# The gate projection of two pairs of each SwiGLU stage by seven products of quarters

## The chip, the cores and the metric

The kernel runs on one core of a Trainium2 chip, in one launch. The metric is the device time of one execution in microseconds. A core has five engines that run side by side, each with its own in-order row of instructions: TensorE (PE; its weight loads are PEld), VectorE (DVE), ScalarE (ACT), GpSimd (POOL) and SyncE (SP), which here only issues DMAs.

## The reference, cut to what matters

```python
D_MODEL, SEQ, DEPTH, D_FF = 1024, 512, 2, 2816

def swiglu_ffn(x, g, w_gate, w_up, w_down):
    h = rmsnorm(x, g)
    return (jax.nn.silu(h @ w_gate) * (h @ w_up)) @ w_down

    for i in range(DEPTH):
        x = x + 0.5 * swiglu_ffn(x, ffn1_norm[i], ffn1_w_gate[i], ffn1_w_up[i], ffn1_w_down[i])
        h = rmsnorm(x, mix_norm[i])
        if i % 2 == 0:
            ...
        else:
            ...
        x = x + 0.5 * swiglu_ffn(x, ffn2_norm[i], ffn2_w_gate[i], ffn2_w_up[i], ffn2_w_down[i])
    return rmsnorm(x, final_norm)
```

All is fp32. So there are four SwiGLU stages, and a mixer (attention of several kinds; left out above) behind the first and behind the third.

## The kernel before

**Numbers in two halves.** An fp32 operand is cut into a high part that TensorE takes and the rest, a low part: `h` by a copy on ScalarE, `l = src - h` on VectorE (`cut`, L326 to L331, or `parts`, L708 to L710). `mm3` (L333 to L336) makes one product from three matmuls: high by high (L334), high by low (L335), low by high (L336). The normalised activations are cut once a stage (tiles `xg`); weights are cut as they come, from `raw` tiles into `wh` and `wl`, four buffers each.

**A stage.** The 2816 columns are 11 pairs `k` of 256, in three groups, `GROUPS` = (0,4), (4,8), (8,11). For each pair of a group `gate_up` (L758 on) makes gate and up; behind the group's pairs `proj_T` makes its part of the down projection, in four steps of 256 rows, each ending in two `update`s of x (L585; `x7` is the last). Each step takes two units of down weights, cut at L329 and L330.

**A pair.** The first one or two pairs of a stage go by `gate_up_pair` and aren't touched. In every other pair the gate is made directly: two units of 512 rows, each 2 x 4 products of 512 columns, 48 matmuls in all, into two PSUM banks of tag `psT`. Behind it come `rb` (the row of 1/rms of the norm), a product with it on VectorE (L780), the Silu on ScalarE (L781) and a product on GpSimd (L782). The up projection goes by `seven` (L688 on), a scheme of the Strassen kind: the 1024 x 256 weights and the activations are split in quarters, and seven products of quarters take the place of eight. It makes four additions of weight quarters (L725 to L728, tiles `s`), and four cuts: h1 (512 columns, product 1), h2 (1024; products 2 and 4), u and v (1024 each, cut from the sums; products 3, 5 and 6, 7). Each product is 4 x 3 matmuls of 256 columns, 84 in all, run in the order 1, 2, 3, 5, 6, 7, 4 into four banks of tag `psG`. Two copies on ScalarE (L742, L746) and seven operations on VectorE (L744 to L756) combine them. The activations' sums (`Sums`, tiles `t7h`, `t7l`) are made once a stage. At the end up is multiplied by gate (L785, L787), and the result is cut for the down projection (`split`, L508 and L509).

**The ahead work.** `cut_ahead` cuts the mixers' weights while the first three stages run their down projections, into which it is woven: load a unit into `craw`, cut it into `ch` (ScalarE, L329) and `cl` (VectorE, L330), store both to DRAM. Each of its loads is held back by a copy on GpSimd (L305) of one column of the x tile updated last, into the `craw` tile:

```python
            if gate:
                nc.gpsimd.tensor_copy(raw[:, 0:1], mark[0])
```

**What sets the order.** The program is written in the order of the loops; a scheduler at build time then sets each engine's row by data and buffers, and the engines run their rows in order, waiting on semaphores. So an instruction that waits holds back all behind it on its engine. All loads and stores of weights are issued in order by SyncE. Buffers of one tag are handed out by the order in which they come free.

Of the kernel before, what the change touches and what calls it, by code (L numbers as in the profile page):

```python
# [20 lines left out]
P = 128  # L21
# [6 lines left out]
GROUPS = ((0, 4), (4, 8), (8, 11))  # L28
PSUM_BUFS = {'B': 4, 'S': 3, 'T': 4, 'C': 2, 'X': 2, 'G': 4}
SB_BUFS = {'xg': 18, 'f': 36, 'm': 8, 'p': 8, 'pt': 9}  # L30
AHEAD = 3
YB = 5
TRAIL = (8, 4)
# [32 lines left out]
def hybrid_kernel(tc, x_in, positions, ffn1_norm, ffn1_w_gate, ffn1_w_up, ffn1_w_down, mix_norm,  # L66
# [4 lines left out]
    with ExitStack() as ctx:  # L71
# [11 lines left out]
        def ps_tile(tag):  # L83
            return psp.tile([P, S], F32, tag=tag, bufs=PSUM_BUFS[tag], name=nm("ps" + tag))

        def tile_(tag, dt=F32R):
            return sb.tile([P, S], dt, tag=tag, bufs=SB_BUFS[tag], name=nm(tag))

# [168 lines left out]
        def wunit(src, a, b, rows=False, key=None, tag=("raw", "wh", "wl")):  # L257

            n = a * b
            if key in cut_units:
                res = []
                for part, t in zip(cut_units[key], tag[1:]):
                    w = sb.tile([P, 1024], F32R, tag=t, bufs=W_BUFS, name=nm(t))
                    nc.sync.dma_start(w[:, :n].bitcast(F32), part)
                    res.append(w[:, :n].rearrange("p (a b) -> p a b", a=a))
                return res
            h, l = cut(load_raw(src, a, b, rows, tag[0], RAW_BUFS), n, tag[1:], W_BUFS)
            return (h[:, :n].rearrange("p (a b) -> p a b", a=a), l[:, :n].rearrange("p (a b) -> p a b", a=a))  # L270
# [414 lines left out]
                        self.term[n][c] = tuple(t[:, sl] for t in self.norm.xg[c + 4 * i])  # L685
                    yield

        def seven(w, f0, sums, z):  # L688

# [37 lines left out]
            for t, ns in ((u, (3, 5)), (v, (6, 7))):  # L729
                h, l = new("wh", F32R, W_BUFS), new("wl", F32R, W_BUFS)  # L730
                parts(h, l, t)
                for i, n in enumerate(ns):
                    st[n] = quarter(h, i), quarter(l, i)
            bank = [ps_tile("G") for _ in range(4)]
            q = {n: bank[i % 4][:, i // 4 * 256:i // 4 * 256 + 256] for i, n in enumerate((1, 2, 3, 5, 6, 7, 4))}
            k1, k3, k6 = (sb.tile([P, 256], F32, tag="k7", bufs=6, name=nm("k7")) for _ in range(3))
            a, b = slice(0, 256), slice(256, 512)
# [20 lines left out]
        def gate_up(wg, wu, k, norm, sums, at):  # L758

            f0 = 256 * k  # L760
            if k < (1 if norm.source is None else 2):
                gate_up_pair(wg, wu, f0, norm, k == 0, sums.work, at)
                return
            psg = [ps_tile("T"), ps_tile("T")]
            for hf in range(2):
                h, l = wunit(wg[hf * 512:(hf + 1) * 512, f0:f0 + 256].rearrange("(c p) f -> p c f", p=P), 4, 256)
                if hf:
                    norm.rstd()
                for f in range(2):
                    if hf and f:  # L770
                        norm.finish()
                    for c in range(4):
                        xh, xl = norm.xg[hf * 4 + c]
                        mm3(psg[f], h[:, c, f * P:(f + 1) * P], l[:, c, f * P:(f + 1) * P], xh, xl,
                            hf == 0 and c == 0, hf == 1 and c == 3)
            rb = norm.rstd_row()
            gs, up = [], [tile_("p", F32) for _ in range(2)]
            for f in range(2):
                g = tile_("p", F32)
                nc.vector.tensor_mul(g, psg[f], rb)  # L780
                nc.scalar.activation(g, g, AF.Silu)  # L781
                nc.gpsimd.tensor_mul(g, g, rb)  # L782
                gs.append(g)
            seven(wu, f0, sums, up)
            nc.vector.tensor_mul(up[0], up[0], gs[0])  # L785
            at.append(split(up[0]))
            nc.vector.scalar_tensor_tensor(up[1], up[1], -1.0, gs[1], op0=ALU.mult, op1=ALU.mult)  # L787
            at.append(split(up[1]))
            mark[0] = at[-1][0][:, 0:1].bitcast(F32)
# [817 lines left out]
```

## Time and profile before

| | |
|---|---|
| median of 3 runs | 2017.05 us (2015.41 to 2019.02) |
| the profiled execution | 2017.72 us |
| its span, first to last instruction | 2016.0 us |
| mean granted clock of TensorE in it | 0.995 of full speed |

The profile is of one execution of its own. The page gives busy times over the span, the chain of work that ended last, and the costliest groups of instructions. A timeline lists an engine's instructions by start, with their length, their line and tiles (out<-in), and in brackets how long the engine had been idle before and what released it. A window gives, for a stretch, the time for which each engine was busy. The eight places that the change touches lie at 146 (stage 1, pair 4), 280 (pair 8), 828 and 960 (stage 2), 1191 and 1321 (stage 3), 1779 and 1906 us (stage 4).

### The profile page before, as it was taken

What the parts mean: (1) busy time and instruction counts of PE and PEld (TensorE: products, weight loads), DVE (VectorE), ACT (ScalarE), POOL (GpSimd) and SP (SyncE); (2) the same over time, 40 slices, a digit from 0 to 9 for tenths busy, and PEclk for the clock granted to TensorE, in tenths of its full rate; (3) what the DMA queues carried; (4) which work ended last, traced back from release to release, by engine and by line L of the source; (5) the groups of instructions that cost most, each with busy time, mean ns of one, the idle gap of its engine ahead of it and who ended that gap; (6) DMA issues with size and microseconds to landing.
All of it is one profiled execution on the core that took longest, in us unless ns stands there. A gap on an engine that the chain in (4) does not pass through costs nothing.

```text
span 2016.0 us, 30453 instructions
## 1 busy us (share of the span) xinstructions
PE 1955.9 (97%) x11575; PEld 1731.1 (86%) x11575; DVE 1391.0 (69%) x2448; ACT 905.8 (45%) x1570; POOL 335.6 (17%) x418
## 2 busy tenths in 40 slices
PE   8999999999989999999999999999999999999998
PEld 7888888898877788788888888888999788889898
DVE  6767767535787786676768758566698787567464
ACT  6434334325677644333445434334346764334143
POOL 1201111023234011111101111010112202011012
PEclk9999999999999999999999999999999999999999
DMA  5386493933100235737543493423542232323321
GB/s 168 94 264 193 137 281 125 335 128 123 46 11 12 64 109 170 246 105 251 182 155 96 144 305 105 135 87 106 197 143 95 78 95 83 116 84 105 104 85 63
DMA packets 216962, 273.58 MB, mean 136 GB/s; under 512 B 25368, under 2 KB 190960, under 8 KB 216816
## 3 DMA queue, kind: packets, MB, share of 16 engines
q1 hardware_dynamic: 209888, 265.23, 40.7%
q10 hardware_dynamic: 6736, 6.37, 1.0%
q8 instruction: 91, 1.49, 0.3%
q14 instruction: 55, 0.45, 0.1%
q0 software_dynamic: 192, 0.04, 0.0%
HBM read 221.72 MB, written 49.87 MB: 135 GB/s over the span
## 4 chain that ended last, share of the span: by engine, by line
PE 52%; DVE 8%; DMA 2%; issue 2%; ACT 1%; POOL 0%; ACTq 0%; POOLq 0%; DVEq 0%; SPq 0%
PE psB L334 6%; PE psB L335 6%; PE psB L336 6%; PE psT L334 6%; PE psT L336 6%; PE psT L335 6%; PE psG L334 4%; PE psG L336 4%; PE psG L335 4%; DMA craw<-in_od_w_in_dram 2%; DVE f L1432 1%; DVE sm L1431 1%; PE psC L964 1%; PE psS L336 1%; PE psS L334 1%
## 5 line engine op out<-in xcount | busy, mean ns | idle before, releaser
L330 DVE TENSOR_TENSOR wl<-raw,wh 128x1024 fp32r<-128x1024 f32 (+1 forms) x210 | 270.2, 1288 | 82.1 <-ACT wh L329 79.3
L329 ACT ACTIVATE wh<-raw 128x1024 fp32r<-128x1024 f32 (+1 forms) x210 | 207.9, 992 | 196.5 <-PE psB L335 119.7
L334 PE MATMUL psT<-xg,wh 128*128 128x512 f32 x704 | 275.1, 391 | 0.0
L335 PE MATMUL psT<-xg,wh 128*128 128x512 f32 x704 | 274.2, 390 | 0.0
L336 PE MATMUL psT<-xg,wl 128*128 128x512 f32 x704 | 274.1, 390 | 0.0
L334 PE MATMUL psB<-f,wh 128*128 128x512 f32 x656 | 255.5, 390 | 0.0
L335 PE MATMUL psB<-f,wh 128*128 128x512 f32 x656 | 255.3, 389 | 0.0
L336 PE MATMUL psB<-f,wl 128*128 128x512 f32 x656 | 255.2, 389 | 0.0
L782 POOL TENSOR_TENSOR p<-p,p 128x512 f32<-128x512 f32 x78 | 132.4, 1700 | 702.5 <-ACT p L781 652.6
L334 PE MATMUL psG<-t7h,wh 128*128 128x256 f32 x624 | 178.9, 287 | 13.7 <-ACT k L742 7.9
L335 PE MATMUL psG<-t7l,wh 128*128 128x256 f32 x624 | 177.3, 284 | 0.0
L336 PE MATMUL psG<-t7h,wl 128*128 128x256 f32 x624 | 176.8, 284 | 0.0
L336 PEld LDWEIGHTS psT<-xg,wl 128*128 128x128 f32 x704 | 132.2, 188 | 27.7
L334 PEld LDWEIGHTS psT<-xg,wh 128*128 128x128 f32 x704 | 132.3, 188 | 26.6
L335 PEld LDWEIGHTS psT<-xg,wh 128*128 128x128 f32 x704 | 132.3, 188 | 26.3
L334 PE MATMUL psB<-wh,xg 128*128 128x256 f32 x512 | 148.5, 290 | 0.3 <-DMA wh<-cuth 0.2
L336 PEld LDWEIGHTS psB<-f,wl 128*128 128x128 f32 x656 | 123.1, 188 | 25.7
L336 PE MATMUL psB<-wh,xg 128*128 128x256 f32 x512 | 145.1, 283 | 0.0
L334 PEld LDWEIGHTS psB<-f,wh 128*128 128x128 f32 x656 | 123.2, 188 | 25.3
L335 PEld LDWEIGHTS psB<-f,wh 128*128 128x128 f32 x656 | 123.2, 188 | 25.1
L335 PE MATMUL psB<-wl,xg 128*128 128x256 f32 x512 | 144.7, 283 | 0.0
L710 DVE TENSOR_TENSOR wl<-s,wh 128x1024 fp32r<-128x1024 f32 x78 | 101.8, 1307 | 57.3 <-ACT wh L709 57.3
(307 smaller groups left out, 4602.1 us busy)
## 6 DMA issues: line engine op xcount, KB each, us to landing
raw<-in_ffn_w_down_dram SPq DMA_DIRECT2D x168, 256.0 KB, 3.3
raw<-in_ffn_w_gate_dram SPq DMA_DIRECT2D x80, 512.0 KB, 4.1
raw<-in_ffn_w_up_dram SPq DMA_DIRECT2D x80, 512.0 KB, 4.1
cuth<-ch SPq DMA_DIRECT2D x40, 512.0 KB, 4.5
cutl<-cl SPq DMA_DIRECT2D x40, 512.0 KB, 4.8
wl<-cutl SPq DMA_DIRECT2D x40, 512.0 KB, 3.6
wh<-cuth SPq DMA_DIRECT2D x40, 512.0 KB, 4.4
craw<-in_od_w_in_dram SPq DMA_DIRECT2D x16, 512.0 KB, 5.2
```

What stands on the lines that cost most here:

```text
L329: pin(nc.scalar.activation(h[:, :n], raw[:, :n], AF.Copy))
L330: pin(nc.vector.tensor_sub(l[:, :n], raw[:, :n], h[:, :n].bitcast(F32)))
L334: nc.tensor.matmul(ps, lh, rh, start=start, stop=False)
L335: nc.tensor.matmul(ps, lh, rl, start=False, stop=False)
L336: nc.tensor.matmul(ps, ll, rh, start=False, stop=stop)
L710: nc.vector.tensor_sub(l, src, h.bitcast(F32))
L782: nc.gpsimd.tensor_mul(g, g, rb)
L964: nc.tensor.matmul(job["accs"][0][:, j * P:512], v(j), hl[j][part], start=first, stop=last)
L1431: nc.vector.max(out=m8, in_=bd[i])
L1432: nc.vector.match_replace(out=bd[i], in_to_replace=m8, in_values=bd[i], imm_value=-3e38)
```

## The change

In pairs 4 and 8, the first pairs of the second and third group, of each stage, the gate is made by `seven` as well, with four banks of tag `psT`. Its result then lies in two tiles `p`, of which the second has its sign turned; so the product with `rb` takes a factor -1 there (L786 of the changed kernel). Silu and the GpSimd product are as before. What `seven` reads of the activations is there already. The weights of a gate are loaded in the same two transfers of 512 KB.

```diff
--- before.py
+++ after.py
@@ -28,6 +28,7 @@
 GROUPS = ((0, 4), (4, 8), (8, 11))
 PSUM_BUFS = {'B': 4, 'S': 3, 'T': 4, 'C': 2, 'X': 2, 'G': 4}
 SB_BUFS = {'xg': 18, 'f': 36, 'm': 8, 'p': 8, 'pt': 9}
+GATE_SEVEN = (4, 8)
 AHEAD = 3
 YB = 5
 TRAIL = (8, 4)
@@ -685,7 +686,7 @@
                         self.term[n][c] = tuple(t[:, sl] for t in self.norm.xg[c + 4 * i])
                     yield
 
-        def seven(w, f0, sums, z):
+        def seven(w, f0, sums, z, tag="G"):
 
 
 
@@ -731,7 +732,7 @@
                 parts(h, l, t)
                 for i, n in enumerate(ns):
                     st[n] = quarter(h, i), quarter(l, i)
-            bank = [ps_tile("G") for _ in range(4)]
+            bank = [ps_tile(tag) for _ in range(4)]
             q = {n: bank[i % 4][:, i // 4 * 256:i // 4 * 256 + 256] for i, n in enumerate((1, 2, 3, 5, 6, 7, 4))}
             k1, k3, k6 = (sb.tile([P, 256], F32, tag="k7", bufs=6, name=nm("k7")) for _ in range(3))
             a, b = slice(0, 256), slice(256, 512)
@@ -761,23 +762,30 @@
             if k < (1 if norm.source is None else 2):
                 gate_up_pair(wg, wu, f0, norm, k == 0, sums.work, at)
                 return
-            psg = [ps_tile("T"), ps_tile("T")]
-            for hf in range(2):
-                h, l = wunit(wg[hf * 512:(hf + 1) * 512, f0:f0 + 256].rearrange("(c p) f -> p c f", p=P), 4, 256)
-                if hf:
-                    norm.rstd()
-                for f in range(2):
-                    if hf and f:
-                        norm.finish()
-                    for c in range(4):
-                        xh, xl = norm.xg[hf * 4 + c]
-                        mm3(psg[f], h[:, c, f * P:(f + 1) * P], l[:, c, f * P:(f + 1) * P], xh, xl,
-                            hf == 0 and c == 0, hf == 1 and c == 3)
+            if k in GATE_SEVEN:
+                psg = [tile_("p", F32) for _ in range(2)]
+                seven(wg, f0, sums, psg, "T")
+            else:
+                psg = [ps_tile("T"), ps_tile("T")]
+                for hf in range(2):
+                    h, l = wunit(wg[hf * 512:(hf + 1) * 512, f0:f0 + 256].rearrange("(c p) f -> p c f", p=P), 4, 256)
+                    if hf:
+                        norm.rstd()
+                    for f in range(2):
+                        if hf and f:
+                            norm.finish()
+                        for c in range(4):
+                            xh, xl = norm.xg[hf * 4 + c]
+                            mm3(psg[f], h[:, c, f * P:(f + 1) * P], l[:, c, f * P:(f + 1) * P], xh, xl,
+                                hf == 0 and c == 0, hf == 1 and c == 3)
             rb = norm.rstd_row()
             gs, up = [], [tile_("p", F32) for _ in range(2)]
             for f in range(2):
-                g = tile_("p", F32)
-                nc.vector.tensor_mul(g, psg[f], rb)
+                g = psg[f] if k in GATE_SEVEN else tile_("p", F32)
+                if k in GATE_SEVEN and f:
+                    nc.vector.scalar_tensor_tensor(g, psg[f], -1.0, rb, op0=ALU.mult, op1=ALU.mult)
+                else:
+                    nc.vector.tensor_mul(g, psg[f], rb)
                 nc.scalar.activation(g, g, AF.Silu)
                 nc.gpsimd.tensor_mul(g, g, rb)
                 gs.append(g)
```

A place gives up 48 matmuls of 512 columns, two cuts of 1024 on ScalarE and VectorE, and two VectorE products from PSUM (L780). It gets 84 matmuls of 256 columns, a cut of 512 and three of 1024, four additions of 512, two copies of 256 on ScalarE, seven combining operations of 256 on VectorE, and two products of 512 from SBUF. Lines of the changed kernel are one higher up to the middle of `seven`'s end and eight higher behind the gate.

The build sets the rows anew. VectorE, stage 3, the end of the down projection of group 1 and pair 4; `cl` is the ahead cut, `wl<-raw` and `wl<-s` cuts of weights and of their sums, `x_99` the last x tile, `k` and `p` the combining operations. Before (`psT` tiles are the gate's results, `wl_11914`, `wl_11924` and `wl_11928` are the up projection's h2, u and v):

```order
L585 SCALAR_TENSOR_TENSOR x_99<-psB_11744,x_99 128x512
L710 TENSOR_TENSOR wl_11914<-raw_11907,wh_11913 128x1024
L710 TENSOR_TENSOR wl_11924<-s_2409_11917,wh_11923 128x1024
L330 TENSOR_TENSOR cl_12699<-craw_11829,ch_12698 128x1024
L780 TENSOR_TENSOR p_11897<-psT_11833,p_10878 128x512
L725 TENSOR_TENSOR s_2444_12125<-raw_12113,raw_12115 128x512
L728 TENSOR_TENSOR s_2445_12126<-raw_12113 128x512
L726 TENSOR_TENSOR s_2445_12126<-s_2444_12125,raw_12113 128x512
L780 TENSOR_TENSOR p_11901<-psT_11834,p_10878 128x512
L727 TENSOR_TENSOR s_2444_12125<-s_2445_12126,raw_12115 128x512
L710 TENSOR_TENSOR wl_11928<-s_2410_11918,wh_11927 128x1024
```

Now (`wl_12234`, `wl_12244` and `wl_12248` are the up projection's h2, u and v; `psT` tiles are the gate's seven products):

```order
L331 TENSOR_TENSOR cl_13019<-craw_12085,ch_13018 128x1024
L751 TENSOR_TENSOR k_2455_12123<-psT_12117,k_2453_12121 128x256
L711 TENSOR_TENSOR wl_12234<-raw_12227,wh_12233 128x1024
L752 TENSOR_TENSOR p_12089<-k_2455_12123,k_2454_12122 128x256
L754 TENSOR_TENSOR k_2455_12123<-psT_12118,k_2455_12123 128x256
L788 TENSOR_TENSOR p_12089<-p_12089,p_11134 128x512
L755 TENSOR_TENSOR p_12090<-psT_12120,k_2455_12123 128x256
L757 TENSOR_TENSOR p_12090<-psT_12119,k_2455_12123 128x256
L711 TENSOR_TENSOR wl_12244<-s_2464_12237,wh_12243 128x1024
L786 SCALAR_TENSOR_TENSOR p_12090<-p_12090,p_11134 128x512
L711 TENSOR_TENSOR wl_12248<-s_2465_12238,wh_12247 128x1024
```

The cuts of h2 and u stood ahead of the ahead cut and now stand behind it, with five of the gate's combining operations and its first product with `rb` among them.

VectorE, stage 1, the same part of the program, before (`cl` are three ahead cuts, `wl_1461` the gate's second unit, `wl_1503` the up projection's h1):

```order
L330 TENSOR_TENSOR wl_1461<-raw_1458,wh_1460 128x1024
L330 TENSOR_TENSOR cl_1369<-craw_1329,ch_1368 128x1024
L585 SCALAR_TENSOR_TENSOR x_98<-psB_1335,x_98 128x512
L585 SCALAR_TENSOR_TENSOR x_99<-psB_1336,x_99 128x512
L330 TENSOR_TENSOR cl_1416<-craw_1376,ch_1415 128x1024
L330 TENSOR_TENSOR cl_2292<-craw_1423,ch_2291 128x1024
L710 TENSOR_TENSOR wl_1503<-raw_1498,wh_1502 128x512
```

Now (`wl_1437`, `wl_1447` and `wl_1451` are the gate's h2, u and v):

```order
L711 TENSOR_TENSOR wl_1437<-raw_1430,wh_1436 128x1024
L331 TENSOR_TENSOR cl_1369<-craw_1329,ch_1368 128x1024
L711 TENSOR_TENSOR wl_1447<-s_283_1440,wh_1446 128x1024
L586 SCALAR_TENSOR_TENSOR x_98<-psB_1335,x_98 128x512
L586 SCALAR_TENSOR_TENSOR x_99<-psB_1336,x_99 128x512
L331 TENSOR_TENSOR cl_1416<-craw_1376,ch_1415 128x1024
L711 TENSOR_TENSOR wl_1451<-s_284_1441,wh_1450 128x1024
L745 TENSOR_TENSOR p_1426<-psT_1455,k_293_1458 128x256
L749 TENSOR_TENSOR k_294_1459<-psT_1457,k_294_1459 128x256
L331 TENSOR_TENSOR cl_2356<-craw_1423,ch_2355 128x1024
```

A cut of the gate's sums now stands ahead of the last two x updates, and the last ahead cut stands behind the gate's first combining operations.

## Rows read from the trace of the kernel before

**Rows 1.** The page: busy time of each engine; shares of the chain that ended last

```profile
PE 1955.9 (97%) x11575; PEld 1731.1 (86%) x11575; DVE 1391.0 (69%) x2448; ACT 905.8 (45%) x1570; POOL 335.6 (17%) x418
PE 52%; DVE 8%; DMA 2%; issue 2%; ACT 1%; POOL 0%; ACTq 0%; POOLq 0%; DVEq 0%; SPq 0%
```

**Rows 2.** Windows: stretch, length, busy PE, PEld, DVE, ACT, POOL (count); clock, DMA, GB/s

```profile
146.25:157.13 10.88, 10.88 (x49) 9.01 (x48) 3.81 (x5) 2.76 (x3) 0.18 (x1) 1.00 1.03 348
157.13:173.17 16.04, 12.40 (x85) 11.63 (x84) 14.02 (x19) 7.51 (x10) 3.13 (x2) 0.89 0.77 260
290.54:302.64 12.10, 10.58 (x86) 10.17 (x84) 10.99 (x16) 6.45 (x9) 3.53 (x2) 1.00 0.92 276
838.54:853.92 15.38, 10.84 (x86) 10.22 (x84) 12.86 (x17) 7.30 (x10) 3.14 (x2) 1.00 0.52 193
971.28:985.69 14.41, 11.92 (x85) 11.42 (x84) 13.09 (x17) 5.46 (x9) 3.76 (x2) 0.88 0.47 161
1201.74:1214.91 13.17, 10.59 (x85) 10.17 (x84) 12.52 (x16) 5.76 (x9) 3.76 (x2) 1.00 0.64 220
1778.74:1789.62 10.88, 10.88 (x50) 9.01 (x48) 6.24 (x8) 2.73 (x3) 0.17 (x1) 1.00 0.16 48
1789.62:1799.69 10.07, 10.07 (x86) 10.07 (x84) 7.57 (x11) 4.92 (x7) 2.95 (x2) 1.00 0.24 60
```

**Rows 3.** Timeline, VectorE, stage 3, pair 4: start, duration, what, [idle before, releaser]

```profile
1202.25 1.23 DVE L330 TENSOR_TENSOR cl<-craw,ch 128x1024 fp32r<-128x1024 f32 x1 [3.65 <-ACT ch L329]
1205.20 1.79 DVE L726 TENSOR_TENSOR s<-s,raw 128x512 f32<-128x512 f32 x1
1207.51 0.68 DVE L727 TENSOR_TENSOR s<-s,raw 128x512 f32<-128x512 f32 x1
1208.11 1.21 DVE L710 TENSOR_TENSOR wl<-s,wh 128x1024 fp32r<-128x1024 f32 x1
1215.19 0.42 DVE L754 TENSOR_TENSOR p<-psG,k 128x256 f32<-128x256 f32 x1
1215.52 0.41 DVE L756 TENSOR_TENSOR p<-psG,k 128x256 f32<-128x256 f32 x1
```

**Rows 4.** The same stretch: ScalarE and GpSimd

```profile
1201.15 1.06 ACT L329 ACTIVATE ch<-craw 128x1024 fp32r<-128x1024 f32 x1 [3.81 <-DMA craw<-in_od_w_out_dram]
1194.70 1.06 POOL L305 COPY craw<-x 128x1 f32<-128x1 f32 x1 [12.26 <-DVE x L585]
1204.82 1.61 POOL L782 TENSOR_TENSOR p<-p,p 128x512 f32<-128x512 f32 x1 [9.06 <-ACT p L781]
```

**Rows 5.** Timelines, stage 2, pair 4 (838 on) and pair 8 (971 on): VectorE and TensorE

```profile
840.14 1.23 DVE L330 TENSOR_TENSOR cl<-craw,ch 128x1024 fp32r<-128x1024 f32 x1 [6.55 <-ACT ch L329]
848.16 0.39 PE L334 MATMUL psG<-t7h,wh 128*128 128x256 f32 x1 [2.72 <-ACT k L742]
972.19 1.22 DVE L330 TENSOR_TENSOR cl<-craw,ch 128x1024 fp32r<-128x1024 f32 x1 [4.06 <-DMA cutl<-cl]
979.44 0.38 PE L334 MATMUL psG<-t7h,wh 128*128 128x256 f32 x1 [2.25 <-ACT k L742]
```

**Rows 6.** TensorE after that wait, and the window of it (columns as in Rows 2)

```profile
982.69 0.41 PE L334 MATMUL psG<-t7h,wh 128*128 128x256 f32 x1
982.90 0.41 PE L335 MATMUL psG<-t7l,wh 128*128 128x256 f32 x1
981.00:983.00 2.00, 1.76 (x9) 1.47 (x8) 2.00 (x4) 0.00 (x0) 0.00 (x0) 0.50 0.17 29
```

**Rows 7.** Timelines, stage 1, pair 4: VectorE, SyncE's issues, TensorE

```profile
145.94 1.28 DVE L585 SCALAR_TENSOR_TENSOR x<-psB,x 128x512 f32<-128x512 f32 x2
155.51 1.23 DVE L330 TENSOR_TENSOR cl<-craw,ch 128x1024 fp32r<-128x1024 f32 x1 [5.80 <-ACT ch L329]
147.99 1.87 SPq L699 DMA_DIRECT2D raw<-in_ffn_w_up_dram  x2
163.97 0.39 PE L334 MATMUL psG<-xg,wh 128*128 128x256 f32 x1 [2.72 <-ACT wh L709]
```

## The prediction

> **What bounds the kernel now.** The page first: TensorE is busy 97% of the span, and no other engine is above 69% except its own weight loads [rows 1]. So the first price of an edit is the TensorE time that it removes, and the second is the idle time that the other 3% hold. The chain that ended last says whose idle time that is: after TensorE's 52% the largest share is VectorE's 8% [rows 1]. The windows then show where it sits. I cut the eight places that the change touches (pairs 4 and 8 of four stages) into the gate projection and the up projection behind it. The gate takes 10.88 us with TensorE busy all of it, at all eight places (the first and one later stand there) [rows 2]. The up projection takes 10.07 us where nothing disturbs it, in the last stage [rows 2]; pair 8 of stage 3 and pair 8 of stage 4 are like it. I call these three the quiet places. At the other five it takes 16.04, 12.10, 15.38, 14.41 and 13.17 us for the same 84 products [rows 2]: 20.7 us are lost behind these five gates, and VectorE is busy 11.0 to 14.0 us there against 7.57. The five are the places beside `cut_ahead`, which cuts the mixer's weights during the down projections of the first three stages.
>
> The timeline of one such place, pair 4 of stage 3, shows the mechanism. GpSimd's small copy that frees the next ahead load waits for the last x update of the down projection and runs at 1194.70. The load lands and ScalarE's half of the cut runs at 1201.15, after 3.81 us of waiting for it [rows 4]. VectorE's half stands in its in-order row and starts at 1202.25 after 3.65 us of idling [rows 3]. All that is queued behind it on VectorE, cuts of the up projection's weights among it, waits too. I call the end of this ahead cut C: 1203.48 here; 841.37 and 973.41 for pairs 4 and 8 of stage 2 [rows 5]; 156.74 for pair 4 of stage 1 [rows 7]. The up projection ends 11.4, 12.6, 12.3 and 16.4 us after its C [rows 2]. C hangs on an x update and a load, not on how fast the gate is multiplied.
>
> **Part 1, TensorE.** The gate loses 48 products of 512 columns, 48 x 0.2267 = 10.88 us, and gets 84 of 256, 84 x 0.1199 = 10.07 us, both from the undisturbed windows [rows 2]. That is 0.81 us a place and 6.5 us for eight. Weight loads are busy all of the 10.07 us [rows 2], so the smaller products don't run at half the time of the larger. The page "TensorE: Matmul & The Clock Gate" of the Trainium skill (section Back-to-back issue gap) puts the isolated gap at N/2.4 + 2.5 ns, so 215.8 and 109.2 ns; the saving would be 1.19 us a place and 9.5 us for eight. The rows are 0.2267 and 0.1199 us, the trace disagrees, and the rows decide.
>
> **Part 2, VectorE's and ScalarE's load.** By the spacing of VectorE's rows, a 1024 cut costs 1.13 us, a 512 operation 0.60, a 256 one 0.33 [rows 3] (the cut from its length of 1.21 less the 0.08 by which a 512 operation of 0.68 exceeds 0.60). A place loses two cuts and two 512 products (3.5 us), and gets three cuts of 1024 and one of 512, four additions, seven combining operations and two 512 products: 4.0 + 2.4 + 2.3 + 1.2 = 9.9 us. So VectorE has 6.4 us more a place, on an engine with idle time; ScalarE gets about 2.4 us (one 1024 cut of 1.06 [rows 4], a 512 cut of about half, two short copies), hidden everywhere by its 45% load [rows 1]. GpSimd and the loads do what they did.
>
> **Part 3, the quiet places.** VectorE is busy 6.24 + 7.57 = 13.8 us in gate and up together [rows 2]. With 6.4 more, less some 3 us of cuts and additions that the new order puts into the down projection before, that is 17.2 of 20.1 us: it fits. The tightest operand is the second unit of sums of the up projection. Its buffers come free when the gate's next-to-last product ends, and its low half stands behind one combining operation: 0.33 + 1.21 = 1.5 us after the gate's end, 2.7 if a GpSimd product blocks it (below), and it is wanted after two products of the up projection, 24 x 0.12 = 2.9 us. So I keep the whole saving: 3 x 0.81 = -2.4 us. The bounds are -2.4 and 0.
>
> **Part 4, the busy places.** Here the order decides. At pair 4 of stage 3, VectorE did the up projection's h2 cut and first cut of sums ahead of the ahead cut. In the changed kernel both stand behind it, with the gate's last five combining operations and its 512 product between them. So the up projection's third product can't have its low half before C + 5 x 0.33 + 0.60 + 1.13 + 1.21 = C + 4.6 us [rows 3], 4.7 with hand-overs, and then 58 of its products of 0.12 us are left, 7.0 us. It ends at C + 11.7.
>
> One thing more falls in this stretch. GpSimd's product of the gate starts about 0.7 us after the gate's first 512 product, beside the cut of sums. In the rows, L726 takes 1.79 us beside the GpSimd product that began at 1204.82, where its like L727 takes 0.68 [rows 3, 4]: 1.1 us. I take 1.1 at each place whose row has it: C + 12.8. Against what was: pair 4 of stage 3 +1.4 us, pair 8 of stage 2 +0.5, pair 4 of stage 2 +0.2. The saving of 0.81 is inside these, since the end no longer hangs on the gate. Bounds are 1.1 less without the block, and 1.4 more with a fall of the clock (rival B).
>
> At pair 4 of stage 1 C itself moves. The x updates ran at 145.94, and both up loads and an ahead load are issued behind them, at 147.99 and just before [rows 7]. The changed order has one of the gate's new cuts (1.13 us) in front of these updates, so C and the up loads come 1.1 us later. Behind C the row is about as long as before (8.5 us to the low half of the third product in both), with one more GpSimd block: 1.1 + 1.1 = +2.2 us, bounds +1.1 and +5 (both added waits in row with the clock). At pair 8 of stage 1, where C is far ahead and 2.0 us are lost [rows 2], no row decides: the saving kept whole gives -0.8, one more block +0.3 to +1.2; I take +0.2, the middle.
>
> The sum: 1.4 + 0.5 + 0.2 + 2.2 + 0.2 = +4.5 at the busy places, -2.4 at the quiet ones, so +2.1 us. The profiled execution took 2017.72 us (span 2016.0 and 1.72 around it), 0.67 above the median; the difference is put on the median: **2019.2 us** (2019.8 against the profiled one).
>
> **Rivals.** B, slower: the new waits take TensorE's clock. In pair 8 of stage 2 TensorE waited 2.25 us [rows 5], and its granted clock then read 0.50 (1.2 GHz instead of 2.4) in the window behind it, with products 0.21 us apart for some 15 of them [rows 6]: 15 x 0.09 = 1.4 us. In pair 4 of stage 1 it waited 2.72 us [rows 7] and the window's clock is 0.89 [rows 2]. Against it: pair 4 of stage 2 waited 2.72 us too [rows 5] and kept 1.00 [rows 2]. In the changed kernel the waits ahead of the second and third products are 2.6 to 3.9 us (gate end 0.81 earlier, C unchanged), with only 12 products between. If each of the five places has one fall more, that is 7.0 us on top: +9.1, **2026.2 us**. It decides from two falls on, since 2.1 + 2.8 = 4.9 us is more than 0.2%.
>
> C, faster: all eight savings are kept, since the ahead cut comes as much earlier as the gate ends earlier: -6.5, **2010.6 us**. For it: VectorE's idling before the ahead cut [rows 3] could hold the moved operations. Against it: the load is gated by the x update, and the row behind the cut is in order.
>
> D: GpSimd's product costs VectorE nothing. The cut of sums starts at C + 3.4 us and that product at about C + 3.7, so VectorE is first; L726, which paid, began 0.38 us after GpSimd [rows 3, 4]. Then four blocks of 1.1 go: 2.1 - 4.4 = -2.3, **2014.8 us**. The page "SBUF — State Buffer" of the Trainium skill (section Who interferes with whom) says that a VectorE instruction with two SBUF inputs contends with GpSimd's reads and that whoever issues first blocks the other; by that rule D holds wherever VectorE is first, and the 1.79 us agrees with its other half.
>
> **How the numbers follow.** The forecast has 0.45, B 0.23, C 0.14, D 0.18. A measurement of this kernel can tell some 0.2% from no change, 4.0 us: 2013.0 to 2021.1. Faster: C and a tail of D (0.03), 0.17. Slower: B and the part of the forecast in which one fall or the upper bound of stage 1 comes on top (0.14), 0.37. Same: the rest, 0.46. The range runs from 2012.0 (most of C, 0.12, outside) to 2027.0 (B's upper part, 0.08, outside).
>
> **What would show it.** Right: gates of 10.07 us at all eight places; up projections of 10.07 at the three quiet ones; at the five others the end of the up projection 12 to 14 us after the end of the ahead cut, with the cut of sums behind it on VectorE. Wrong: up projections at the quiet places above 10.4 us (part 3); C moved earlier by 0.8 at the busy ones (C holds); the cuts of sums at 1.2 us where GpSimd runs (D); stretches with products 0.21 us apart at three or more places (B).

## The result, and the profile after

The changed kernel takes 2034.94 us (median of 4 runs, 2034.37 to 2037.28) against 2018.01 us for the kernel before beside it (4 runs). The ratio is 1.0084, 95% interval 1.0070 to 1.0098: 17 us slower. The forecast was 2019.2 us in a range of 2012.0 to 2027.0: the time lies outside it, on the side of rival B.

The page of the changed kernel, the line of busy times and that of the chain:

```profile
PE 1965.2 (97%) x11863; PEld 1751.5 (86%) x11863; DVE 1442.7 (71%) x2552; ACT 923.5 (45%) x1602; POOL 335.2 (16%) x418
PE 39%; DVE 8%; issue 7%; DMA 3%; ACT 1%; POOL 1%; SPq 0%; ACTq 0%; POOLq 0%; DVEq 0%
```

TensorE is busy 9 us more than before [rows 1], though each of the eight gates has 0.81 us less to do: lengths at a low clock count as busy. VectorE is busy 51.7 us more, 6.5 a place, as part 2 of the prediction had it. The chain has 7% of "issue" where it had 2%.

Windows of the changed kernel, columns as in [rows 2]: gate and up of stage 1, pair 4; up of stage 1, pair 8; up of stage 2, pairs 4 and 8; gate, up and the next pair's up of stage 3, pair 4; gate, up and the next pair's up of stage 3, pair 8, a quiet place:

```profile
147.63:158.22 10.59, 10.23 (x86) 10.03 (x84) 6.45 (x8) 4.33 (x6) 0.18 (x1) 1.00 1.03 342
158.22:178.25 20.03, 13.89 (x85) 13.16 (x85) 17.44 (x26) 7.60 (x10) 3.78 (x2) 0.74 0.66 221
294.81:314.12 19.31, 14.24 (x87) 13.03 (x86) 16.41 (x24) 7.62 (x10) 2.91 (x2) 0.73 0.77 238
850.38:867.60 17.22, 13.26 (x86) 12.55 (x85) 15.34 (x22) 8.43 (x11) 3.66 (x2) 0.80 0.54 186
985.12:1001.83 16.71, 13.26 (x87) 12.56 (x85) 14.12 (x19) 8.43 (x11) 3.68 (x2) 0.80 0.59 199
1207.26:1218.95 11.69, 10.62 (x86) 10.21 (x84) 8.72 (x13) 4.09 (x8) 1.06 (x1) 1.00 0.87 303
1218.95:1232.09 13.14, 10.59 (x87) 10.18 (x85) 12.95 (x17) 7.32 (x11) 3.69 (x2) 1.00 0.67 234
1242.99:1254.50 11.51, 10.58 (x85) 10.17 (x84) 9.68 (x14) 4.77 (x7) 2.76 (x2) 1.00 0.20 57
1340.01:1350.08 10.07, 10.07 (x85) 10.07 (x84) 6.38 (x11) 4.41 (x6) 0.00 (x0) 1.00 0.23 61
1350.08:1360.16 10.08, 10.08 (x86) 10.08 (x85) 10.08 (x13) 5.56 (x8) 3.63 (x2) 1.00 0.31 95
1371.07:1381.67 10.60, 10.47 (x86) 10.16 (x84) 9.94 (x14) 5.29 (x8) 3.04 (x2) 1.00 0.17 55
```

The quiet gate takes 10.07 us and its up 10.08, as forecast. In the up projections of the busy places the granted clock is 0.74, 0.73, 0.80, 0.80 and 1.00, where before it was 1.00 at three of them and 0.89 and 0.88 at two [rows 2]. Two things weren't in the forecast: four gates beside ahead work are longer than 10.07 us (10.59 and 11.69 above; 10.30 and 11.03 at stage 2, pairs 4 and 8), and the up projection of the *next* pair is longer too (11.51 and 10.60 above). At the quiet place VectorE is busy 10.08 of 10.08 us: it has nothing left to give in that stretch.

From the lengths of TensorE's stretches in both profiles (gate and up together, then the next pair's up):

| place | forecast | gate and up | next pair's up |
|---|---|---|---|
| stage 1, pair 4 | +2.2 | +3.7 | 0.0 |
| stage 1, pair 8 | +0.2 | +6.4 | -0.2 |
| stage 2, pair 4 | +0.2 | +1.3 | 0.0 |
| stage 2, pair 8 | +0.5 | +2.5 | +0.2 |
| stage 3, pair 4 | +1.4 | +0.8 | +1.4 |
| three quiet places | -2.4 | -2.4 | +1.0 |
| sum | +2.1 | +12.3 | +2.4 |

That is 14.7 of the 17.5 us by which the spans differ (2033.5 and 2016.0). The other 2.8 lie in stretches whose code is the same, such as 1.4 us ahead of the first of the eight places. One caution: at a busy place the same code varies by some 5 us between profiles. The up projection of stage 2, pair 8 took 14.41 us before, and 11.43 to 16.79 us in four experiments that leave that place as it was. The 6.4 us of stage 1, pair 8 came back in an experiment of its own. For stages 2 and 3, three profiles of the two kernels and the experiments below have the change, and five don't, with these places and their ahead work otherwise as here. Gate, up projection and next up projection take together, on average, 37.1 against 36.8 us at stage 2, pair 4; 37.0 (35.6 to 38.0) against 34.4 (32.4 to 38.2) at stage 2, pair 8; and 36.6 (36.3 to 36.9) against 34.1 (33.0 to 35.7) at stage 3, pair 4. So the loss at stage 3 stands clear of the scatter, that at stage 2, pair 8 is likely, and the 1.3 us of stage 2, pair 4 can't be told from nothing.

**Stage 1, pair 8**, the largest loss, from the timelines. First the kernel before: GpSimd's copy that frees the held ahead load, the ahead store behind that load on SyncE, SyncE's issue of the up projection's second half of weights, and ScalarE's cut of it.

```profile
281.96 0.18 POOL L305 COPY craw<-x 128x1 f32<-128x1 f32 x1 [10.85 <-DVE x L585]
282.59 0.50 SPq L283 DMA_DIRECT2D cutl<-cl  x1
283.13 0.43 SPq L699 DMA_DIRECT2D raw<-in_ffn_w_up_dram  x1
288.59 1.06 ACT L709 ACTIVATE wh<-raw 128x1024 fp32r<-128x1024 f32 x1 [2.79 <-DMA raw<-in_ffn_w_up_dram]
```

The changed kernel: the same four, then VectorE (with a GpSimd product among its rows), TensorE's third product with its first low half, and a window.

```profile
286.99 1.06 POOL L306 COPY craw<-x 128x1 f32<-128x1 f32 x1 [10.06 <-ACT wh L710]
288.48 2.03 SPq L284 DMA_DIRECT2D cutl<-cl  x1
290.56 0.43 SPq L700 DMA_DIRECT2D raw<-in_ffn_w_up_dram  x1
295.59 1.06 ACT L710 ACTIVATE wh<-raw 128x1024 fp32r<-128x1024 f32 x1 [2.71 <-DMA raw<-in_ffn_w_up_dram]
293.59 1.22 DVE L331 TENSOR_TENSOR cl<-craw,ch 128x1024 fp32r<-128x1024 f32 x1 [4.65 <-DMA cutl<-cl]
295.51 0.69 DVE L726 TENSOR_TENSOR s<-raw,raw 128x512 f32<-128x512 f32 x1 [0.37 <-DMA raw<-in_ffn_w_up_dram]
300.12 0.68 DVE L728 TENSOR_TENSOR s<-s,raw 128x512 f32<-128x512 f32 x1
300.72 1.75 DVE L786 SCALAR_TENSOR_TENSOR p<-p,p 128x512 f32<-128x512 f32 x1
303.28 1.27 POOL L790 TENSOR_TENSOR p<-p,p 128x512 f32<-128x512 f32 x1 [1.35 <-ACT p L789]
303.34 3.43 DVE L711 TENSOR_TENSOR wl<-s,wh 128x1024 fp32r<-128x1024 f32 x2
302.01 0.58 PE L335 MATMUL psG<-xg,wh 128*128 128x256 f32 x1 [1.88 <-ACT wh L710]
305.68 0.58 PE L337 MATMUL psG<-xg,wl 128*128 128x256 f32 x1 [0.45 <-DVE wl L711]
302.00:304.00 2.00, 1.23 (x4) 0.93 (x4) 2.00 (x4) 1.43 (x2) 0.72 (x1) 0.50 0.80 250
```

The gates began at 279.66 and 284.74. So the load was issued 3.5 us into the gate before and 5.8 us now, and its cut ran at +8.9 and +10.9 us. Of the 2.35 us between the issues, GpSimd's copy has 0.9 (1.06 us for 0.18, beside a VectorE cut that had begun at 286.79) and the store's issue 1.5 (2.03 us for 0.50). Three of VectorE's four additions for the sums need this load too: the first now runs at 295.51, behind the ahead cut of 293.59, and the sum that ScalarE waits for (L728) at 300.12, after the gate's combining operations, its first product with the norm's row, and the up projection's h2 cut. The third product starts at 302.01, 7.2 us after the gate's end, against 3.6 before. Its low half is the first of the two cuts of sums at 303.34. They take 3.43 us together where their spacing gives 2.34, beside the GpSimd product that began 0.06 us ahead of them, and TensorE gets the low half at 305.68. The clock is at half (1.2 GHz) by then, 0.50 in the window.

Against the gate's start the second load's cut came 1.9 us later than before, the sums' first cut on ScalarE 2.8, the first matmul with the third product's low half 4.4 (it began at 296.17 before), and the end 6.4. Read along this chain, 1.9 us are the load, 2.5 the rows behind it, and 2.0 the products behind, at the lower clock. That is a reading of one profile; no run takes the three apart.

**Stages 2 and 3**, VectorE in the changed kernel: ahead cut, cut of sums, and the gate's second product with the norm's row, for pair 4 of stage 2 and of stage 3; last, GpSimd's product there:

```profile
852.16 1.23 DVE L331 TENSOR_TENSOR cl<-craw,ch 128x1024 fp32r<-128x1024 f32 x1 [5.07 <-ACT ch L330]
857.23 1.21 DVE L711 TENSOR_TENSOR wl<-s,wh 128x1024 fp32r<-128x1024 f32 x1
858.36 1.76 DVE L786 SCALAR_TENSOR_TENSOR p<-p,p 128x512 f32<-128x512 f32 x1
1219.04 1.23 DVE L331 TENSOR_TENSOR cl<-craw,ch 128x1024 fp32r<-128x1024 f32 x1 [2.79 <-ACT ch L330]
1223.77 1.21 DVE L711 TENSOR_TENSOR wl<-s,wh 128x1024 fp32r<-128x1024 f32 x1
1224.90 1.78 DVE L786 SCALAR_TENSOR_TENSOR p<-p,p 128x512 f32<-128x512 f32 x1
1223.93 2.20 POOL L790 TENSOR_TENSOR p<-p,p 128x512 f32<-128x512 f32 x1 [9.51 <-ACT p L789]
```

The cut of sums ends 5.05 and 4.71 us after the ahead cut (forecast 4.7); it takes 1.21 us and is not held up by GpSimd, whose product begins 0.16 us after it. L786 behind it is: 1.76 and 1.78 us where the like product L788 took 0.68 at stage 1, pair 8.

### The profile page after: what moved, and what is told of

Read it like the earlier page. It is cut to its first block, busy times and chain, and to the rows that moved or that the text cites. A ratio compares the mean times of both kernels' runs of the same rounds, so it can differ in the third digit from the quotient of the medians.

```text
span 2033.5 us, 31192 instructions
## 1 busy us (share of the span) xinstructions
PE 1965.2 (97%) x11863; PEld 1751.5 (86%) x11863; DVE 1442.7 (71%) x2552; ACT 923.5 (45%) x1602; POOL 335.2 (16%) x418
## 4 chain that ended last, share of the span: by engine, by line
PE 39%; DVE 8%; issue 7%; DMA 3%; ACT 1%; POOL 1%; SPq 0%; ACTq 0%; POOLq 0%; DVEq 0%
PE psB L335 4%; PE psB L336 4%; PE psB L337 4%; PE psT L335 4%; PE psT L336 4%; PE psT L337 4%; PE psG L335 4%; PE psG L337 4%; PE psG L336 4%; DVE f L1440 1%; DMA craw<-in_od_w_in_dram 1%; DVE sm L1439 1%; DMA craw<-in_od_w_out_dram 1%; DVE wl L711 1%; DVE p L939 1%
## 5 line engine op out<-in xcount | busy, mean ns | idle before, releaser
L331 DVE TENSOR_TENSOR wl<-raw,wh 128x1024 fp32r<-128x1024 f32 (+1 forms) x194 | 249.6, 1288 | 61.5 <-ACT wh L330 58.9
L330 ACT ACTIVATE wh<-raw 128x1024 fp32r<-128x1024 f32 (+1 forms) x194 | 190.9, 986 | 172.9 <-PE psB L336 94.7
L335 PE MATMUL psT<-xg,wh 128*128 128x512 f32 (+1 forms) x672 | 252.8, 376 | 0.0
L336 PE MATMUL psT<-xg,wh 128*128 128x512 f32 (+1 forms) x672 | 251.9, 375 | 0.0
L337 PE MATMUL psT<-xg,wl 128*128 128x512 f32 (+1 forms) x672 | 251.8, 375 | 0.0
L711 DVE TENSOR_TENSOR wl<-s,wh 128x1024 fp32r<-128x1024 f32 x94 | 118.9, 1266 | 53.9 <-ACT wh L710 53.8
L710 ACT ACTIVATE wh<-s 128x1024 fp32r<-128x1024 f32 x94 | 98.7, 1055 | 119.9 <-PE psT L336 88.6
L337 PE MATMUL psG<-xg,wl 128*128 128x256 f32 x468 | 136.9, 292 | 11.5 <-DVE wl L711 11.5
L337 PEld LDWEIGHTS psT<-xg,wl 128*128 128x128 f32 x672 | 126.7, 189 | 22.7
L335 PEld LDWEIGHTS psT<-xg,wh 128*128 128x128 f32 x672 | 126.9, 189 | 21.8
L336 PEld LDWEIGHTS psT<-xg,wh 128*128 128x128 f32 x672 | 126.9, 189 | 21.8
```

Source lines behind the costliest of these rows:

```text
L330: pin(nc.scalar.activation(h[:, :n], raw[:, :n], AF.Copy))
L331: pin(nc.vector.tensor_sub(l[:, :n], raw[:, :n], h[:, :n].bitcast(F32)))
L335: nc.tensor.matmul(ps, lh, rh, start=start, stop=False)
L336: nc.tensor.matmul(ps, lh, rl, start=False, stop=False)
L337: nc.tensor.matmul(ps, ll, rh, start=False, stop=stop)
L710: nc.scalar.activation(h, src, AF.Copy)
```

## Experiments

The place of a stage is told by a counter `stage[0]`, raised where a stage begins. Ratios are to the kernel before, timed beside each; four kernels (told below) ran once and are read for their traces. Each diff shows the lines that matter.

**The quiet places alone.**

```diff
-GATE_SEVEN = (4, 8)
+GATE_SEVEN = ((3, 8), (4, 4), (4, 8))
+            sv = (stage[0], k) in GATE_SEVEN
-            if k in GATE_SEVEN:
+            if sv:
```

> The gate by seven products only at the three quiet places (stage 3 pair 8, stage 4 pairs 4 and 8); the five busy places as in the kernel before. By the trace of the changed kernel each of the three gates is 0.81 us shorter and two of the next pairs' up projections are 0.5 us longer: -2.4 + 1.0 = -1.4 us, so 2016.6 beside 2018.0. My forecast for these places was -2.4 (2015.6). If the loss of 17 us came from VectorE's added load wherever it falls, a share of it (3 of 8 places, +6) would show here.

2018.49 us (12 runs), ratio 0.9994, interval 0.9982 to 1.0005. In the trace three gates of 10.07 us and next up projections 0.40 and 0.33 us longer: -1.7 us. The estimate fits, and no share of the 17 us is here; it is too small to tell from nothing.

**Stage 1, pair 8 alone** (the same edit, with `((1, 8),)`).

> The gate by seven products only at stage 1 pair 8, where the trace of the changed kernel has the largest loss (gate -0.81, up projection +7.2). If the place makes its own loss (its loads are issued behind an ahead load that waits for the x update, and its row of VectorE behind the ahead cut): +6.4 us, 5 to 8. If the loss is carried over from pair 4 of the same stage, which shifted the ahead work: -0.8 to +1.

2022.53 us (10 runs), ratio 1.0014, interval 1.0004 to 1.0025: +2.8 us, short of the 5 to 8. In the trace the gate is 0.81 us shorter and the up projection 7.59 longer, 19.69 us: +6.8, and the next one 0.2 shorter. The rest of the run gave some of it back at places with unchanged code (stage 2, pair 8 was 3.0 us shorter). The place makes its loss by itself; the whole shows less than the place, by the scatter told above.

**The clock kept up with idle products** (the flag `warm` is set for the up projections of the five busy places).

```diff
             for n in (1, 2, 3, 5, 6, 7, 4):
+                x1 = sums.term[1][0][0]
+                for _ in range({2: 12, 3: 16}.get(n, 0) if warm else 0):
+                    pin(nc.tensor.matmul(q[n], x1[:, 0:P], x1, start=True, stop=True))
                 for c in range(4):
```

> The changed kernel with 12 idle products of 256 columns before the second and 16 before the third product of the up projection at the five busy places (28 x 0.12 = 3.4 us of TensorE's time a place, written to a bank that the real product overwrites). If lost clock is the larger part (14.5 us of the five up projections are time at the lower clock: their length less 10.07 and less the waits): the clock stays up, the idle products lie in the waits, -8 to -13 us, so 2022 to 2027. If the waits alone matter, no gain, or up to 17 us slower where the idle products lie on the path.

2033.48 us (4 runs), ratio 1.0070, interval 1.0052 to 1.0088. The whole run's clock, from the list of cores:

```profile
core 0: 2033.1 us, clock 0.995
```

It was 0.987 without them. The clock stayed at 1.00 in four of the five up projections (0.91 in the fifth), and the time didn't follow: it is 1.5 us less by the medians, 2.8 by the ratios. The five up projections became 4.3 us shorter together (82.1 against 86.4 us, idle products included), but their gates grew by 0.9 us and the next pairs' up projections by 3.3 (11.57 and 11.27 at stage 2 where they had been 10.07 and 10.29). There TensorE waits for VectorE's combining operations, 0.65 and 0.64 us at stage 2. Of the 4.3 us, 3.9 are at pair 8 of stage 1, where in this build the third product's low half also came 2.5 us earlier after the gate's start.

The idle products could have eaten the gain themselves. At stages 2 and 3 the third product begins right behind them, but its low half had been cut on VectorE only 0.25, 0.26 and 0.92 us before its first use, and a later product waits for VectorE at all three places (0.99, 0.97 and 0.30 us). The first of these waits:

```profile
861.22 0.39 PE L336 MATMUL psG<-t7h,wh 128*128 128x256 f32 x1 [0.99 <-DVE p L749]
```

So the low clock went along with the loss, and over the whole run it was not what set it; what it is worth at single places, pair 8 of stage 1 above all, isn't shown.

**The ahead loads held back by x5 instead of x7**, with the change and without it.

```diff
-            mark[0] = x[c][:, 0:1]
+            if c < 6:
+                mark[0] = x[c][:, 0:1]
```

> The changed kernel with the ahead loads held back by the x tile of the last step but one (x5) instead of the last (x7), so that neither the ahead cut nor the up projection's loads wait for the end of the down projection. If the ahead cut and the loads behind the last x update make the loss: the up projections at the busy places fall to 10 to 13 us, 10 to 25 us faster than the changed kernel, 2010 to 2025. If VectorE's load makes it: within 3 us of 2035.

2019.70 us (10 runs), ratio 0.9998, interval 0.9986 to 1.0011: 15 us less than the changed kernel. Windows of the up projections at the five places, in the order of the stages:

```profile
157.88:178.20 20.32, 13.77 (x84) 13.02 (x85) 17.44 (x25) 7.59 (x10) 3.78 (x2) 0.75 0.64 216
294.76:311.01 16.25, 13.73 (x87) 12.93 (x85) 14.81 (x22) 6.43 (x9) 5.08 (x2) 0.79 0.73 235
848.03:858.11 10.08, 10.08 (x86) 10.08 (x85) 10.08 (x13) 5.42 (x8) 3.69 (x2) 1.00 0.66 227
977.41:987.78 10.37, 10.34 (x86) 10.13 (x85) 10.27 (x14) 5.37 (x8) 3.69 (x2) 1.00 0.61 205
1205.61:1215.78 10.17, 10.17 (x86) 10.13 (x85) 10.07 (x14) 5.37 (x8) 3.70 (x2) 1.00 0.76 272
```

In stages 2 and 3 they fall to 10.08, 10.37 and 10.17 us at full clock, but in stage 1 they stay at 20.3 and 16.3. And the wait doesn't vanish altogether: the three gates there take 11.01, 12.13 and 11.29 us, and the next pairs' up projections 10.8 to 11.9.

> The kernel before, with the ahead loads held back by x5 instead of x7: what the earlier mark is worth without the change. If the wait for the last x update also made the losses of before at the busy places of stages 2 and 3 (5.3, 4.3 and 3.1 us over 10.07): about 10 us faster than before, 2008, and the change under x5 then costs some 10 us, nearly all at the two places of stage 1. If the mark only matters with the change: 2018, and the change under x5 costs 1 to 2 us.

2013.46 us (10 runs), ratio 0.9973, interval 0.9962 to 0.9983: half of what the first theory wanted. So under x5 the change costs 5 to 6 us instead of 17.

**The six places of stages 2 to 4, under x5.**

> The changed kernel with x5 as the mark and the gate by seven products at six places, those of stages 2 to 4; stage 1 as before. The trace with all eight places under x5 has +8.4 us in stage 1 and -6.6 after it. If places are independent: 2018.4 less some 7 to 10 us, 2008 to 2011. Against the kernel before with x5: if six places by seven products are worth anything there, 1 to 3 us faster; if the gain is eaten by the next pairs (their up projections 0.5 to 1.8 us longer), the same.

2013.32 us (11 runs), ratio 0.9976, interval 0.9966 to 0.9986: the same as the kernel before under x5, and not the 2008 to 2011 of independent places. The six up projections take 10.08 us each, but the gates of stage 2 take 12.85 and 15.42 us (2.4 and 3.6 us of waiting in them) and that of stage 3, pair 4 11.62. The wait went from the up projection into the gate.

**No ahead work in stage 1**, with the change and without it; one run each.

```diff
-                ffn(n1, ffn1_w_gate[0], ffn1_w_up[0], ffn1_w_down[0], nm_, hook(), ev_ahead, 2, load_early)
-                run(ev_ahead)
+                ffn(n1, ffn1_w_gate[0], ffn1_w_up[0], ffn1_w_down[0], nm_, hook(), iter(()), 2, load_early)
```

> The changed kernel without ahead work in stage 1: the first mixer cuts its weights itself, so the whole is some tens of us slower; what is read is stage 1. If the ahead work (its loads and stores ahead of the up projection's loads, its cut ahead of theirs on VectorE) makes the loss there: gates and up projections of pairs 4 and 8 at 10.1 us each, against 20.0 and 19.3 for up now. If VectorE's load by the change itself is too much: still 12 us or more.

> The kernel before without ahead work in stage 1, for comparison with the one above: up projections of pairs 4 and 8 at 10.1 us instead of 16.0 and 12.1, and the two gates at 10.9; so the changed kernel should be 1.6 us shorter in stage 1 beside it if the ahead work is all of the loss.

2007.80 and 2007.68 us. The windows of gate and up at pairs 4 and 8 of stage 1, with the change:

```profile
147.67:157.74 10.07, 10.07 (x85) 10.07 (x84) 6.37 (x11) 4.42 (x6) 0.00 (x0) 1.00 0.25 64
157.74:167.82 10.08, 10.08 (x86) 10.08 (x85) 10.08 (x14) 5.56 (x8) 3.69 (x2) 1.00 0.29 91
274.69:284.76 10.07, 10.07 (x85) 10.07 (x84) 6.38 (x11) 4.41 (x6) 0.00 (x0) 1.00 0.24 62
284.76:294.84 10.08, 10.08 (x86) 10.08 (x85) 10.08 (x14) 5.55 (x8) 3.63 (x2) 1.00 0.31 98
```

10.07 and 10.08 us at both. Without the change it is 10.88 and 10.07 at both. So all of the 10.1 us that the change cost at these two places hangs on the ahead work. Both kernels are 10 us faster than the kernel before, where I had expected them to be slower: what the first mixer loses by cutting its weights itself is less than what stage 1 gains.

**The ahead work of stage 1 reduced to its transfers**, with the change and without it; one run each.

```diff
-                now = key, n, cut(raw, n, ("ch", "cl"), 2)
+                now = key, n, cut(raw, n, ("ch", "cl"), 2) if cuts else (raw, raw)
```

> The changed kernel with the ahead work of stage 1 reduced to its transfers: each unit is loaded (held back by x7 as before) and the loaded numbers are stored twice without being cut, so the first mixer's weights aren't cut rightly and its output isn't the reference's. VectorE and ScalarE have no ahead cut in stage 1; SyncE's row and the traffic stay. If the up projection's loads, issued behind the held ahead load and landing in full queues, make the loss: up at pairs 4 and 8 still 14 to 20 us. If the in-order row behind the ahead cut makes it: 10 to 12 us at both.

> The kernel before with the same reduction (the first mixer's weights aren't cut rightly). Up projections at pairs 4 and 8 of stage 1, 16.0 and 12.1 us before: near 10.1 if the ahead cuts made those too, unchanged if the loads did.

2018.96 and 2010.72 us. In both the loaded numbers are stored without being cut, so the first mixer doesn't get its weights in two halves. The up projections of the changed kernel, pairs 4 and 8 of stage 1:

```profile
157.29:167.37 10.08, 10.08 (x87) 10.08 (x85) 10.08 (x13) 5.56 (x8) 3.87 (x3) 1.00 0.88 258
286.31:296.39 10.08, 10.08 (x87) 10.08 (x85) 10.08 (x13) 5.55 (x8) 3.69 (x2) 1.00 0.96 274
```

10.08 us at full clock, with the DMA engines busy 0.88 and 0.96 of the time; without the change 10.07. So traffic alone doesn't make the loss. But the two rows aren't told apart as cleanly as I wanted: the build also issues the up projection's loads earlier here, at pair 8 both 17 us ahead of the gate, no longer behind the held ahead load. My guess, not shown, is that the ahead cuts hold up ScalarE's and VectorE's cuts of the stage's own weights, and with them the raw buffers that later loads wait for. The next pairs' up projections are 12.45 and 11.53 us with the change, 11.91 and 10.07 without.

**No ahead work at all**, without the change and with it (`od_ahead` is left out in the same way).

> The kernel before without any ahead work: both mixers cut their weights themselves. All eight places are quiet: up projections at 10.1 us, 20.7 us less there; what the mixers lose without it decides the total, 2000 to 2030.

> The changed kernel without any ahead work. If the ahead work makes all of the loss, all eight places behave as the quiet ones: eight gates shorter by 0.81 (-6.5 us) and the next pair's up projection 0.5 us longer at up to seven of them (+3.5): 3 us faster than the kernel before without ahead work (by 0.15%). If VectorE's load limits by itself, as slow or slower.

1993.72 us, ratio 0.9875 (0.9857 to 0.9892), and 1991.96 us, ratio 0.9864 (0.9848 to 0.9879), 4 runs each: the two fastest versions tried, and faster than the 2000 to 2030 that I had expected. With the change, windows of the gate and up of stage 2, pair 4 and of the next pair's up:

```profile
812.93:823.00 10.07, 10.07 (x86) 10.07 (x84) 6.41 (x11) 2.78 (x5) 0.00 (x0) 1.00 0.30 80
823.00:833.08 10.08, 10.08 (x87) 10.08 (x85) 10.00 (x13) 5.36 (x8) 3.81 (x2) 1.00 0.25 78
843.99:854.44 10.45, 10.33 (x86) 10.12 (x85) 9.79 (x14) 5.17 (x8) 3.16 (x2) 1.00 0.18 53
```

All eight gates take 10.07 us and all eight up projections behind them 10.08, also where ahead work had been. The next pairs' up projections take 10.37 to 10.67 at seven places, 2.8 us together. That leaves -6.5 + 2.8 = -3.7 us at the eight places and behind them. The medians differ by 1.8 us and the ranges overlap (1993.06 to 1995.74 and 1989.65 to 1994.91). The two profiled executions go the other way, with spans of 1991.3 us without the change and 1992.8 with it, lost in stretches whose code is the same. So the change gains at its own places, and a gain of the whole is not shown.

**Both mends together**: no ahead work in stage 1 and x5, without the change, and with it at the five places that are quiet then.

> The kernel before without ahead work in stage 1 and with the ahead loads of stages 2 and 3 held back by x5: the two edits that each gained (some 10 and 5 us) together. If they are independent, 2002 to 2005.

> The same with the gate by seven products at the five places that have no ahead work beside them then (both of stage 1, pair 8 of stage 3, both of stage 4): five gates of -0.81 and four longer up projections of +0.4 behind them, -2.4 us beside the run without; 0 if a longer wait moves elsewhere.

2000.89 us, ratio 0.9907 (0.9891 to 0.9922), and 1997.80 us, ratio 0.9890 (0.9872 to 0.9907), 4 runs each. The mends add up, and a little more: 2002 to 2005 was expected of the first. The five gates take 10.07 us each and four next up projections are 0.3 to 0.6 us longer, as expected; an unchanged place (stage 2, pair 4) took 12.96 us in one and 17.99 in the other, so the difference of 3.1 us between the times is not that of the five places alone.

## Why the prediction was wrong, step by step

**The mechanism was right in the main.** The loss sits at the busy places, behind the ahead work; where that is gone, the eight places are quiet. TensorE's saving of 0.81 us a gate is what the quiet places and all eight without ahead work show, and the estimate of 1.19 us from the formula of the page "TensorE: Matmul & The Clock Gate" of the Trainium skill (section Back-to-back issue gap) is not borne out.

**Part 1, the gate at all eight places.** It took for granted that operands are in time. At three busy places the gate waited for the low half of its own sums on VectorE (10.30, 11.03 and 11.69 us), and at pair 4 of stage 1 its seven products took their 10.07 us, but TensorE then waited 0.35 us for the first cut of the up projection's weights (10.59). One of these waits, at stage 3:

```profile
1214.43 0.39 PE L337 MATMUL psT<-t7h,wl 128*128 128x256 f32 x1 [0.99 <-DVE wl L711]
```

This price, 3.3 us over the four times 10.07, was missing.

**Part 2, "on an engine with idle time".** VectorE's 6.4 us more a place were costed at nothing, by an average. In gate and up projection of a quiet place together VectorE is busy 16.5 of 20.15 us, where part 3 had 17.2 of 20.1; but in the window of a quiet up projection alone it is busy 10.08 of 10.08 us, and what doesn't fit falls on the next pair: +0.3 to +0.6 us at a quiet place, up to +1.4 at a busy one. I stopped the sum at the end of the place. The way from one pair to the next shows at stage 4, pair 4. VectorE frees the weight buffers later, so the next pair's second up load is issued 6.0 us into its gate instead of 3.8, and VectorE then idles 2.10 us for it, against 0.76 before. So part 3's -2.4 us were made and 1.0 us of them was given back behind.

**Part 4, stages 2 and 3.** The row was read rightly: the third product's low half was ready 4.7 to 5.05 us after the ahead cut. Two sizes in the sum were wrong and nearly cancel. The GpSimd block of 1.1 us did not fall on the cut of sums (1.21 us) but on L786 behind it, and TensorE had no further wait in these up projections; in this rival D was right, and so was the rule of the page "SBUF — State Buffer" of the Trainium skill (section Who interferes with whom), that the one who issues first has the port. (At stage 1, pair 8, GpSimd began 0.06 us ahead, and there the block did fall on the cut of sums.) And the products behind ran at half clock at two of three places: from the ready low half to the end 9.2 and 8.3 us at stage 2, 7.1 at stage 3, against 7.0 in the sum. C itself moved by -0.4, +1.7 and +0.4 us against the gate's start; I had it fixed.

**Part 4, stage 1: the step that failed.** At pair 8 the forecast was +0.2 with bounds of -0.8 and +1.2, "no row decides", and it was +6.4: 6.2 of the 15.4 us that the sum lacked. I had looked at VectorE's row only from the gate's end on. The rows that decide were to be had: in the kernel before as in the changed one the up projection's second load stands behind the held ahead loads and a store on SyncE, and three of the four additions wait for it on VectorE, behind the ahead cut. A place without a row got narrow bounds when it ought to have got those of its neighbours (+1.1 to +5 at pair 4). At pair 4 I had C later by 1.1 us and it was 0.3; the row behind C was to be as long as before plus one block, 9.6 us to the third product's low half, and was 11.5, with two blocks (L786 1.76 and L728 1.75 us) and ScalarE's cuts of the sums waiting for the last addition.

**Rival B** came nearest in time and in its sign (+9.1 us). TensorE's busy time over 10.07 us in the five up projections, most of it at the low clock, grew from 6.0 to 14.9 us, by 8.9 where B had 7.0. But as a cause it falls: with the clock kept up by idle products the time fell by 1.5 to 2.8 us of 17. The low clock went along with the waits. Rival C is refuted: against the gate's start C came 0.3 to 1.7 us later at four places and 0.4 earlier at one, nowhere by the gate's 0.81.

What stays open: how much of stage 1's loss is the late load and how much the row of VectorE, beyond the reading of one profile above, since taking the ahead cuts away moved the loads as well; and whether the change gains in the whole without ahead work, where its own places say 3.7 us and the times don't reach that far.

## What to carry to other kernels

Before an engine is called idle, look at its busy time in the very windows that the change fills, and follow its backlog past the end of the place into the next one. In-order rows make one late operand everybody's wait: where work for later is woven into a stage, list for each engine and queue what stands behind it, DMA issues included, before any edit is priced by its own length. And ask whether the woven work pays at all: leaving it out was worth 1.25% here, more than any edit beside it.

## What the runs showed of the hardware

A low granted clock can go along with a loss without setting it: 28 idle products a place brought the whole run's clock from 0.987 to 0.995 and the time from 2034.9 to 2033.5 us only. And GpSimd's product held up VectorE only where it had begun first: L786, L728 and L726 took 1.75 to 1.79 us then, the cuts of sums that began 0.16 us ahead of it their usual 1.21, and the pair of cuts that began 0.06 us behind it 1.1 us more than usual. It holds the other way round too: GpSimd's copy of one column took 1.06 us at stage 1, pair 8, to 0.04 us past the end of a VectorE cut of sums that had begun 0.20 us before it, and 0.18 us in the kernel before, where VectorE ran nothing beside it.
